# Where VectorE sums the w_down jobs: behind the gate of the tile whose loads theirs followed, in written order

## The chip, the cores and the metric

The kernel runs on one core of a Trainium2 chip. TensorE (PE) multiplies, ScalarE (ACT) and VectorE (DVE) work on tiles in on-chip memory, SyncE (SP) and GpSimd (POOL) issue the DMAs here, each in the order of its own queue. The metric is the device time of one launch in microseconds (us); lower is better. All engines run their instructions in the order that the scheduler gave them when the program was built. A line such as L881 is a line of the kernel before.

## The reference

One layer of a hybrid decoder in float32: 256 tokens, model width 2048.

```
h = RMSNorm(x);  z = h @ W_in             # split over three mixers
y = concat(pool_mixer, mla, memory_attn) @ W_o;  x = x + y
h2 = RMSNorm(x)
g = h2 @ W_gate                           # 2048 x 5632
gc = conv_b + sum_j conv_w[j] * shift(g)  # causal, width 3
x = x + (silu(gc) * (h2 @ W_up)) @ W_down # W_down: 5632 x 2048
```

The change touches only the last part, the gated feed-forward layer, and there the stage that makes gate and up.

## The kernel before, in words

Every float32 weight is split into a high part, rounded for TensorE, and a low part, the remainder. ScalarE makes the high part (`wh`, L102) and VectorE the low part (`wl`, L103, raw minus high). A product takes three rounds: high by high, high by low, low by high.

**The stage of gate and up.** The 5632 hidden features are 44 tiles of 128. For each tile f the program loads 1 MB of W_gate and 1 MB of W_up (`load_w`, L89, buffers `wr`, three of them in turn), splits each in two halves of 1024 columns (`wh` and `wl`, four buffers each), and runs 48 matmuls for gate and 48 for up (`gemm_pair`, L166). Gate runs its 32 high ones first and then its 16 low ones; up runs its 16 low ones first and then the 32 high ones. Tiles 1 to 43 go this way. "The start of tile f" below is its first gate matmul.

**The gate operations** (`glu`). VectorE scales the gate out of its accumulator (`g`, L827), ScalarE does the last tap of the convolution (L829), VectorE the other two (L831, twice), ScalarE the silu (L832), VectorE multiplies by up (L848, or L837 in pairs that are multiplied the plain way). Tiles are taken in pairs of an even and an odd one. Most pairs later go through a seven-product scheme: after the odd tile VectorE makes four sums (L852), ScalarE and VectorE split the result (L855, L856).

**The jobs.** The seven-product scheme needs four differences of blocks of W_down. For 28 pieces of 1 MB these are made during the gate and up stage, where the load queue has room: `job_load` (L874) issues the load of a piece into one of two buffers `wj` on SP's queue, `job_sums` subtracts on VectorE (L881, four instructions) and writes the result to a scratch tensor `tsum` with two DMAs on POOL's queue (L883). Job loads follow the loads of tiles 2, 3, 4, 6, 7, 9, 10, 12, 13, 15, 16, 17, 19, 20, 22, 23, 25, 26, 28, 29, 30, 32, 33, 35, 36, 38, 39 and 41. A `wj` buffer is free for the job after next as soon as its `tsum` DMAs have landed; so that job's load waits, on SP's queue, for these. After this stage the down stage (L929 to L931) reads the pieces of W_down and `tsum`.

**What sets the order.** A scheduler orders the instructions of each engine by when it reckons their inputs ready. `keep` pins an instruction behind the one that was written just before it on the same engine. The loads of tiles 1 to 43 and of the jobs are pinned on SP's queue: gate of f, up of f, the job's piece, gate of f+1. The operations of `glu` and `job_sums` are not pinned before the change, although `job_sums` of the piece loaded with tile f is written behind the `glu` of tile f+1.

Of the kernel before, what the change touches and what calls it, by code (L numbers as in the profile page):

```python
# [15 lines left out]
ALU = mybir.AluOpType  # L16
# [48 lines left out]
def layer(ctx, tc, xT_d, xn_d, memT_d, vec_d, tab_d, w_z_d, w_mqkr_d, w_q_d, w_kv_d, w_mem_d, w_pool_d, w_o_d,  # L65
          w_g_d, w_u_d, w_dn_d, out_d):
    nc = tc.nc
# [8 lines left out]
    def nm(s):  # L76
        uid[0] += 1
        return f"{s}_{uid[0]}"

    def ps_main():  # L80
        return psm.tile([P, 512], F32, tag="m", name=nm("psm"))
# [4 lines left out]
    def load_w(src, n, cut=STG, kept=False):  # L86
        raw = stage.tile([P, STG], F32, tag="wr", name=nm("wr"), bufs=3)
        for c in range(0, n, cut):
            keep(nc.sync.dma_start(raw[:, c:min(n, c + cut)], src[:, c:min(n, c + cut)]), kept)  # L89
        return raw[:]  # L90

    def keep(ins, on=True):

        return tc.keep_in_program_order(ins) if on else ins

    def split_w(raw, o, n, cut=HS, kept=False, shift=0):

        hi = stage.tile([P, HS + 64], F32R, tag="wh", name=nm("wh"), bufs=4)[:, shift:shift + HS]
        lo = stage.tile([P, HS + 64], F32R, tag="wl", name=nm("wl"), bufs=4)[:, shift:shift + HS]
        for c in range(0, n, cut):  # L100
            e = min(n, c + cut)
            keep(nc.scalar.copy(hi[:, c:e], raw[:, o + c:o + e]), kept)  # L102
            keep(nc.vector.tensor_tensor(lo[:, c:e], raw[:, o + c:o + e], hi[:, c:e].bitcast(F32), op=ALU.subtract),  # L103
                 kept)
        return hi, lo
# [7 lines left out]
    def rounds(act, k, low):  # L113

        m = act(k)
        h, l = (m[:, 0], m[:, 1]) if len(m.shape) == 3 else (m[:, 0:T], m[:, T:2 * T])
        return (h,) if low else (h, l)
# [37 lines left out]
    def gemm_pair(pss, raws, act):  # L155

        nk = HS // P
        for s, (ps, raw) in enumerate(zip(pss, raws)):


            parts = [split_w(raw, c * HS, HS, shift=16 if c else 48) for c in range(KD // nk)]
            for low in ((False, True) if s == 0 else (True, False)):
                for k in range(KD):
                    i = k % nk
                    for a, m in enumerate(rounds(act, k, low)):
                        nc.tensor.matmul(ps, parts[k // nk][low][:, i * P:(i + 1) * P], m,  # L166
                                         start=k + a == 0 and low == (s == 1), stop=k == KD - 1 and low == (s == 0),
                                         skip_group_check=True)
# [17 lines left out]
    def split_act(dst, src, scale=None, kept=False):  # L186


        h, l = (dst[:, 0], dst[:, 1]) if len(dst.shape) == 3 else (dst[:, 0:T], dst[:, T:2 * T])
        if scale is None:  # L190
            nc.scalar.copy(h, src)
            nc.vector.tensor_tensor(l, src, h.bitcast(F32), op=ALU.subtract)
        else:
            keep(nc.scalar.activation(h, src, AF.Copy, scale=scale), kept)
            keep(nc.vector.scalar_tensor_tensor(l, src, scale, h.bitcast(F32), op0=ALU.mult, op1=ALU.subtract), kept)
# [4 lines left out]
    def v(name, i=0):  # L200
        o = VOFF[name] + i
        return vec[:, o:o + 1]
# [323 lines left out]
    for m in range(6):  # L526
# [5 lines left out]
        a = zs[:, m // 4, :]  # L532
# [273 lines left out]
    r1 = const.tile([P, T], F32, name="r1")  # L806
# [17 lines left out]

    def glu(f, psg, psu, home=None):
        g = fp.tile([P, T], F32, tag="g", name=nm("g"), bufs=1)
        nc.vector.tensor_tensor(g[:], psg, r1[:], op=ALU.mult)  # L827
        gc = fp.tile([P, T], F32, tag="gc", name=nm("gc"), bufs=1)
        nc.scalar.activation(gc[:], g[:], AF.Identity, bias=v("conv_b", f), scale=v("cw2", f))  # L829
        for d, w in ((1, "cw1"), (2, "cw0")):  # L830
            nc.vector.scalar_tensor_tensor(gc[:, d:T], g[:, 0:T - d], v(w, f), gc[:, d:T], op0=ALU.mult, op1=ALU.add)  # L831
        nc.scalar.activation(gc[:], gc[:], AF.Silu)  # L832
        j, e = f // 2, f % 2
        if j not in SEVEN:
            if e == 0:
                aT[j] = fp.tile([P, 2, 2 * T], F32R, name=nm("aT"))
            nc.vector.tensor_tensor(gc[:], psu, gc[:], op=ALU.mult)  # L837
            split_act(aT[j][:, e, :], gc[:])
            return
        if e == 0:  # L840
            aT[j] = (home if j == PAIRS - 1 else away() if j in AWAY
                     else fp.tile([P, 14, P], F32R, name=nm("aS"))[:])
            hold[j] = fp.tile([P, 8, P], F32, tag="s8", name=nm("s8"), bufs=1)
        elif home is not None:
            aT[j] = home
        s = hold[j]
        o = 0 if e else 6
        nc.vector.tensor_tensor(s[:, o:o + 2, :].rearrange("p a t -> p (a t)"), psu, gc[:], op=ALU.mult)  # L848
        if e:
            for d, a, op, b in ((2, 7, ALU.add, 1), (3, 2, ALU.subtract, 6), (4, 6, ALU.subtract, 7),  # L850
                                (5, 0, ALU.subtract, 3)):
                nc.vector.tensor_tensor(s[:, d, :], s[:, a, :], s[:, b, :], op=op)  # L852
            hi, lo = (aT[j][:, i:i + 7].rearrange("p a t -> p (a t)") for i in (0, 7))
            sf = s[:, 0:7, :].rearrange("p a t -> p (a t)")
            nc.scalar.copy(hi, sf)  # L855
            nc.vector.tensor_tensor(lo, sf, hi.bitcast(F32), op=ALU.subtract)  # L856
            if j in AWAY:
                nc.gpsimd.dma_start(forms[:, AWAY.index(j)], aT[j])
# [4 lines left out]
    def away():  # L863
        return fp.tile([P, 14, P], F32R, tag="aL", name=nm("aL"), bufs=1)[:]
# [3 lines left out]
    def job_place():  # L868
        return fp.tile([P, STG], F32, tag="wj", name=nm("wj"), bufs=2)[:]

    def job_load(i):

        raw = job_place()
        keep(nc.sync.dma_start(raw, w_dn_d[SUMMED[i]]))  # L874
        return i, raw

    def job_sums(i, raw):

        r = raw.rearrange("p (b n) -> p b n", n=NN)
        for d, a, b in ((1, 0, 1), (0, 2, 0), (2, 2, 1), (3, 3, 2)):  # L880
            nc.vector.tensor_tensor(r[:, d], r[:, a], r[:, b], op=ALU.subtract)  # L881
        for h in range(2):
            nc.gpsimd.dma_start(tsum[:, i, h * HS:(h + 1) * HS], raw[:, h * HS:(h + 1) * HS])  # L883

    job_at = {2 + i * (KF - 5) // (len(SUMMED) - 1): i for i in range(len(SUMMED))}
    job = None

    raws = [load_w(w[0], STG) for w in (w_g_d, w_u_d)]
    pss = [ps_main()[:, 0:T] for _ in range(2)]
# [6 lines left out]
    for ps, raw in zip(pss, raws):  # L896
        gemm_t(ps, raw, HS, h2, range(8, KD), first=False)
    glu(0, *pss)
    for f in range(1, KF):
        pss = [ps_main()[:, 0:T] for _ in range(2)]  # L900
        gemm_pair(pss, [load_w(w[f], STG, kept=True) for w in (w_g_d, w_u_d)], h2)
        if f < KF - 1:
            glu(f, *pss)
        if job is not None:
            job_sums(*job)
        job = job_load(job_at[f]) if f in job_at else None

# [3 lines left out]
    dn = big.tile([P, 12, NN], F32, tag="act", name="dn")  # L913
    aS = big.tile([P, 14, P], F32R, tag="act2", name="aS")
    glu(KF - 1, *pss, aS[:])
    cnt = [0]

# [202 lines left out]
```

## Time and profile before

| what | value |
|---|---|
| median of three runs | 1013.21 us (1011.52 to 1016.26) |
| the profiled execution | 1012.18 us, span 1010.4 us |
| PE busy | 993.7 us, 98% |
| DVE busy | 785.0 us, 78% |
| ACT busy | 567.5 us, 56% |
| matmuls of L166, first start to last start | 303.9 to 788.4 us |
| DMA over the span | 292 GB/s |

The span is the profiled part of the launch; the rest of the launch's time (1.8 us here) lies around it. A busy share is an average over all stages. For this kernel it says that TensorE is the engine to look at, and that what can be won lies in the few us in which it stood still; which those are is read from the waits and the timeline.

### The profile page before, as it was taken

Reading aid. Unit: us, or ns where it says so; the run is one execution under the profiler, and the core shown is the slowest. Engines: PE = TensorE matmul, PEld = TensorE weight load, DVE = VectorE, ACT = ScalarE, POOL = GpSimd, SP = SyncE. Lnnn points to the kernel's source line nnn. Section 1 sums busy time; section 2 is a strip of 40 time slices with the busy share of each in tenths; the row PEclk is TensorE's granted clock in tenths of the full one; section 3 lists DMA queues with packets and bytes.
Section 4 is the critical chain, followed back from the end, with each engine's and each line's share of the span. In section 5 each row is a group of like instructions: output and inputs, shape, how many; then the busy total and the mean of one; then the engine's idle time right before and its main releaser. Section 6 shows DMA issues by size and latency. Waiting matters only on the chain.

```text
span 1010.4 us, 17323 instructions
## 1 busy us (share of the span) xinstructions
PE 993.7 (98%) x6870; PEld 917.5 (91%) x6870; DVE 785.0 (78%) x1174; ACT 567.5 (56%) x779; POOL 52.1 (5%) x102
## 2 busy tenths in 40 slices
PE   9999999999999999999999999999999999999998
PEld 7899988888889999999999999899999888888886
DVE  6878588765658687777878777777786889989887
ACT  7677666544555454444554444544455666757763
POOL 1100000000100000000000000000010000000000
PEclk9999999999999999999999999999999999999999
DMA  9867445334648799798998979898898999999992
GB/s 360 296 249 278 151 133 202 125 126 149 229 165 305 295 329 343 275 343 304 352 334 318 335 260 333 303 350 318 305 397 339 353 398 362 363 340 394 368 395 101
DMA packets 50578, 294.89 MB, mean 292 GB/s; under 512 B 5696, under 2 KB 6208, under 8 KB 25024
## 3 DMA queue, kind: packets, MB, share of 16 engines
q1 hardware_dynamic: 37728, 242.52, 65.9%
q0 software_dynamic: 12336, 50.47, 12.7%
q8 instruction: 54, 0.88, 0.3%
q10 hardware_dynamic: 432, 0.79, 0.3%
q14 instruction: 28, 0.23, 0.1%
HBM read 255.61 MB, written 38.14 MB: 291 GB/s over the span
## 4 chain that ended last, share of the span: by engine, by line
PE 66%; DVE 14%; DMA 14%; issue 3%; ACT 3%; SPq 0%; DVEq 0%; ACTq 0%
PE psm L166 17%; DMA wj<-in_w_dn 9%; DVE wl L103 8%; PE psm L182 5%; PE psm L184 5%; PE psm L183 5%; PE psm L149 4%; PE psa L931 4%; PE psm L931 4%; PE psa L930 4%; PE psa L929 4%; PE psm L930 4%; PE psm L929 4%; DMA tsum<-wj 2%; PE psm L133 2%
## 5 line engine op out<-in xcount | busy, mean ns | idle before, releaser
L103 DVE TENSOR_TENSOR wl<-wr,wh 128x1024 fp32r<-128x1024 f32 (+2 forms) x344 | 396.5, 1162 | 97.4 <-ACT wh L102 91.2
L102 ACT CAST wh<-wr 128x1024 fp32r<-128x1024 f32 (+2 forms) x344 | 336.0, 1000 | 130.1 <-PE psm L183 49.3
L166 PE MATMUL psm<-h,wh 128*128 128x256 f32 x2752 | 321.5, 277 | 2.1 <-ACT wh L102 2.1
L166 PEld LDWEIGHTS psm<-h,wh 128*128 128x128 f32 x2752 | 317.6, 189 | 2.3 <-ACT wh L102 2.3
L166 PE MATMUL psm<-h,wl 128*128 128x256 f32 x1376 | 169.0, 279 | 8.3 <-DVE wl L103 8.1
L166 PEld LDWEIGHTS psm<-h,wl 128*128 128x128 f32 x1376 | 161.8, 189 | 11.5 <-DVE wl L103 11.3
L881 DVE TENSOR_TENSOR wj<-wj 128x512 f32<-128x512 f32 x112 | 77.1, 688 | 56.0 <-DMA wj<-in_w_dn 54.5
L829 ACT ACTIVATE gc<-g,vec 128x256 f32<-128x256 f32 x44 | 26.5, 603 | 122.8 <-DVE g L827 122.8
L832 ACT ACTIVATE gc<-gc 128x256 f32<-128x256 f32 x44 | 18.4, 418 | 78.9 <-DVE gc L831 78.9
L102 ACT CAST wh<-wj 128x1024 fp32r<-128x1024 f32 (+1 forms) x48 | 47.1, 982 | 22.1 <-PE psa L930 11.6
L103 DVE TENSOR_TENSOR wl<-wj,wh 128x1024 fp32r<-128x1024 f32 (+1 forms) x48 | 53.7, 1133 | 6.3 <-ACT wh L102 2.4
L883 POOL DMA_DIRECT2D tsum<-wj x56 | 29.9, 534 | 398.8 <-DVE wj L881 335.4
L831 DVE SCALAR_TENSOR_TENSOR gc<-g,vec,gc 128x255 f32<-128x255 f32 x88 | 42.2, 479 | 1.3 <-ACT gc L829 0.7
L103 DVE TENSOR_TENSOR wl<-dn,wh 128x1024 fp32r<-128x1024 f32 (+1 forms) x36 | 40.1, 1133 | 3.4 <-ACT wh L102 1.7
L102 ACT CAST wh<-dn 128x1024 fp32r<-128x1024 f32 (+1 forms) x36 | 35.3, 982 | 10.7 <-PE psa L930 4.9
L182 PE MATMUL psm<-wh,cat 128*128 128x512 f32 x96 | 38.1, 397 | 0.0
L184 PE MATMUL psm<-wl,cat 128*128 128x512 f32 x96 | 37.4, 390 | 0.0
L183 PE MATMUL psm<-wh,cat 128*128 128x512 f32 x96 | 37.4, 389 | 0.0
L929 PE MATMUL psa<-wh,aS 128*128 128x512 f32 x84 | 32.7, 389 | 0.0
L930 PE MATMUL psm<-wh,aS 128*128 128x512 f32 x84 | 32.7, 389 | 0.0
L930 PE MATMUL psa<-wh,aS 128*128 128x512 f32 x84 | 32.7, 389 | 0.0
L929 PE MATMUL psm<-wh,aS 128*128 128x512 f32 x84 | 32.7, 389 | 0.0
(247 smaller groups left out, 1439.5 us busy)
## 6 DMA issues: line engine op xcount, KB each, us to landing
wr<-in_w_g SPq DMA_DIRECT2D x44, 1024.0 KB, 7.3
wr<-in_w_u SPq DMA_DIRECT2D x44, 1024.0 KB, 5.4
wj<-in_w_dn SPq DMA_DIRECT2D x32, 1024.0 KB, 8.7
tsum<-wj POOLq DMA_DIRECT2D x56, 512.0 KB, 7.8
wr<-in_w_o SPq DMA_DIRECT2D x16, 1024.0 KB, 4.8
wr<-in_w_dn SPq DMA_DIRECT2D x16, 768.0 KB, 7.1
wr<-tsum SPq DMA_DIRECT2D x12, 1024.0 KB, 7.3
wj<-tsum SPq DMA_DIRECT2D x12, 1024.0 KB, 7.0
```

The lines of the kernel that those rows point to most:

```text
L102: keep(nc.scalar.copy(hi[:, c:e], raw[:, o + c:o + e]), kept)
L103: keep(nc.vector.tensor_tensor(lo[:, c:e], raw[:, o + c:o + e], hi[:, c:e].bitcast(F32), op=ALU.subtract), kept)
L149: keep(nc.tensor.matmul(ps, parts[k // nk][low][:, i * P:(i + 1) * P], m, start=k + a == 0 and low == low_first, stop=k == KD - 1 and low ...
L166: nc.tensor.matmul(ps, parts[k // nk][low][:, i * P:(i + 1) * P], m, start=k + a == 0 and low == (s == 1), stop=k == KD - 1 and low == (s ...
L182: keep(nc.tensor.matmul(ps, xh, hi[:, i, o], start=first and i == 0, stop=False), kept)
L183: keep(nc.tensor.matmul(ps, xl, hi[:, i, o], start=False, stop=False), kept)
L184: keep(nc.tensor.matmul(ps, xh, lo[:, i, o], start=False, stop=last and i == nk - 1), kept)
L831: nc.vector.scalar_tensor_tensor(gc[:, d:T], g[:, 0:T - d], v(w, f), gc[:, d:T], op0=ALU.mult, op1=ALU.add)
L881: nc.vector.tensor_tensor(r[:, d], r[:, a], r[:, b], op=ALU.subtract)
L929: nc.tensor.matmul(ps, a[0], b[0], start=first, stop=False)
L930: nc.tensor.matmul(ps, a[1], b[0], start=False, stop=False)
L931: nc.tensor.matmul(ps, a[0], b[1], start=False, stop=last)
```

## The change

Three things are changed in the loop over the tiles. The first gate operation of every tile (`g`, L827) is pinned behind the instruction written before it, which is the tile's last low-part split. The four subtractions of a job are pinned, each behind the one before, and the first behind the last VectorE operation of `glu`. And `job_sums` of the piece that was loaded with tile f is written behind the `glu` of tile f itself, not of tile f+1; its load stands at the same place in SP's queue.

```diff
     def glu(f, psg, psu, home=None):
         g = fp.tile([P, T], F32, tag="g", name=nm("g"), bufs=1)
-        nc.vector.tensor_tensor(g[:], psg, r1[:], op=ALU.mult)
+        keep(nc.vector.tensor_tensor(g[:], psg, r1[:], op=ALU.mult))
...
         for d, a, b in ((1, 0, 1), (0, 2, 0), (2, 2, 1), (3, 3, 2)):
-            nc.vector.tensor_tensor(r[:, d], r[:, a], r[:, b], op=ALU.subtract)
+            keep(nc.vector.tensor_tensor(r[:, d], r[:, a], r[:, b], op=ALU.subtract))
...
     job_at = {2 + i * (KF - 5) // (len(SUMMED) - 1): i for i in range(len(SUMMED))}
-    job = None
...
         gemm_pair(pss, [load_w(w[f], STG, kept=True) for w in (w_g_d, w_u_d)], h2)
+        job = job_load(job_at[f]) if f in job_at else None
         if f < KF - 1:
             glu(f, *pss)
         if job is not None:
             job_sums(*job)
-        job = job_load(job_at[f]) if f in job_at else None
```

No instruction is added or taken away, and TensorE's order is the same. What moves is VectorE's order and, with it, ScalarE's and POOL's. The tile of a row is told by its buffers: the numbers rise with the program's text.

VectorE, before, around the sums of the job loaded with tile 13 (`wj_4852`), which has its first sum ahead of the gate split of tile 13 (`wr_4716`) and ahead of `g` of tile 12 (`psm_4584`):

```order
L881 TENSOR_TENSOR wj_4852<-wj_4852 128x512
L103 TENSOR_TENSOR wl_4721<-wr_4716,wh_4720 128x1024
L827 TENSOR_TENSOR g_4702<-psm_4584,r_2938 128x256
L103 TENSOR_TENSOR wl_4725<-wr_4716,wh_4724 128x1024
L831 SCALAR_TENSOR_TENSOR gc_4704<-g_4702,vec,gc_4704 128x255
L881 TENSOR_TENSOR wj_4852<-wj_4852 128x512
L831 SCALAR_TENSOR_TENSOR gc_4704<-g_4702,vec,gc_4704 128x254
L881 TENSOR_TENSOR wj_4852<-wj_4852 128x512 x2
L103 TENSOR_TENSOR wl_4777<-wr_4718,wh_4776 128x1024
```

VectorE, with the change, around the sums of the same job (`wj_4838`), which stand behind the pair's last operation (L856) and among the gate split of tile 15 (`wr_4990`) and `g` of tile 14 (`psm_4860`):

```order
L103 TENSOR_TENSOR wl_4923<-wr_4864,wh_4922 128x1024
L848 TENSOR_TENSOR s_661_4712<-psm_4721,gc_4842 128x256
L852 TENSOR_TENSOR s_661_4712<-s_661_4712 128x128
L103 TENSOR_TENSOR wl_4927<-wr_4864,wh_4926 128x1024
L852 TENSOR_TENSOR s_661_4712<-s_661_4712 128x128 x2
L856 TENSOR_TENSOR aS_4711<-s_661_4712,aS_4711 128x896
L881 TENSOR_TENSOR wj_4838<-wj_4838 128x512
L103 TENSOR_TENSOR wl_4995<-wr_4990,wh_4994 128x1024
L881 TENSOR_TENSOR wj_4838<-wj_4838 128x512
L827 TENSOR_TENSOR g_4978<-psm_4860,r_2938 128x256
L881 TENSOR_TENSOR wj_4838<-wj_4838 128x512
L103 TENSOR_TENSOR wl_4999<-wr_4990,wh_4998 128x1024
```

The sums of an odd tile's job have moved from the gate split of the tile itself to that of two tiles on; those of an even tile's job go to the up split of the next tile.

VectorE, before, where it makes the gate split of tile 18 (`wr_5400`) with `g` of tile 17 (`psm_5258`) between its halves:

```order
L852 TENSOR_TENSOR s_723_5248<-s_723_5248 128x128
L103 TENSOR_TENSOR wl_5325<-wr_5262,wh_5324 128x1024
L103 TENSOR_TENSOR wl_5405<-wr_5400,wh_5404 128x1024
L827 TENSOR_TENSOR g_5376<-psm_5258,r_2938 128x256
L103 TENSOR_TENSOR wl_5409<-wr_5400,wh_5408 128x1024
L831 SCALAR_TENSOR_TENSOR gc_5378<-g_5376,vec,gc_5378 128x255
```

The same place with the change (`wr_5406`, `psm_5264`), one of the three places where a job's load stands two tiles, not three, behind the load that used the same buffer:

```order
L881 TENSOR_TENSOR wj_5246<-wj_5246 128x512
L852 TENSOR_TENSOR s_724_5256<-s_724_5256 128x128
L881 TENSOR_TENSOR wj_5246<-wj_5246 128x512 x2
L827 TENSOR_TENSOR g_5384<-psm_5264,r_2938 128x256
L831 SCALAR_TENSOR_TENSOR gc_5386<-g_5384,vec,gc_5386 128x255
L831 SCALAR_TENSOR_TENSOR gc_5386<-g_5384,vec,gc_5386 128x254
L103 TENSOR_TENSOR wl_5411<-wr_5406,wh_5410 128x1024
L848 TENSOR_TENSOR s_724_5256<-psm_5265,gc_5386 128x256
```

Here the gate operations of tile 17 now stand ahead of the gate split of tile 18; the sums of job 16 stand ahead of both.

## The prediction

> **What bounds the kernel now.** I read the page first, for the engine that is busy all the time.
>
> ```profile
> span 1010.4 us, 17323 instructions
> PE 993.7 (98%) x6870; PEld 917.5 (91%) x6870; DVE 785.0 (78%) x1174; ACT 567.5 (56%) x779; POOL 52.1 (5%) x102
> ```
>
> TensorE bounds it, and only what makes it wait can be won. The change moves work in the gate and up stage alone, so the next view is TensorE's timeline there (start, duration, tile, count).
>
> ```profile
> 320.17 3.79 PE L166 MATMUL psm<-h,wl 128*128 128x256 f32 x32
> 323.80 7.42 PE L166 MATMUL psm<-h,wh 128*128 128x256 f32 x64
> 331.05 3.79 PE L166 MATMUL psm<-h,wl 128*128 128x256 f32 x32
> ...
> 781.25 3.79 PE L166 MATMUL psm<-h,wl 128*128 128x256 f32 x32
> ```
>
> From one low-part row to the next is an undisturbed tile: 331.05 - 320.17 = 10.88 us, of which 32 matmuls take 3.63 and 64 take 7.25. Gate is therefore 3.63 + 1.81 = 5.44 us and up another 5.44. The first row is tile 2, the last is tile 43: 461.08 us for 41 tiles that would need 446.08. So **15.0 us** are lost in this stage, and that is all the change can win. Next, who waits for whom between 316 and 789 us (total, times, longest).
>
> ```profile
> PE psm L166 <- DVE wl L103: 8.1, 10, 2.2
> ...
> DVE wj L881 <- DMA wj<-in_w_dn: 54.5, 15, 4.9
> ...
> SPq L874 <- DMA tsum<-wj: 10.5, 3, 7.5
> ```
>
> TensorE stands still for low parts alone, and VectorE waits longest for the job pieces. The timeline of tile 13, which starts at 438.55, shows how the two hang together.
>
> ```profile
> 428.65 0.37 SPq L874 DMA_DIRECT2D wj<-in_w_dn  x1
> ...
> 437.60 0.69 DVE L881 TENSOR_TENSOR wj<-wj 128x512 f32<-128x512 f32 x1 [3.44 <-DMA wj<-in_w_dn]
> 438.21 1.22 DVE L103 TENSOR_TENSOR wl<-wr,wh 128x1024 fp32r<-128x1024 f32 x1
> 439.35 0.42 DVE L827 TENSOR_TENSOR g<-psm,r 128x256 f32<-128x256 f32 x1
> ...
> 443.77 1.23 DVE L103 TENSOR_TENSOR wl<-wr,wh 128x1024 fp32r<-128x1024 f32 x1 [0.15 <-ACT wh L102]
> 445.05 1.21 PE L166 MATMUL psm<-h,wl 128*128 128x256 f32 x8 [0.90 <-DVE wl L103]
> 446.85 1.19 PE L166 MATMUL psm<-h,wl 128*128 128x256 f32 x8 [0.59 <-DVE wl L103]
> ```
>
> The first subtraction stands at the head of VectorE's queue before its piece is there (9 us after the issue). Behind it wait the gate split, `g`, all of the gate chain, then the up split at 443.77, which TensorE needs at 444.15 and has at 445.05. VectorE, not the load of weights, was late.
>
> **The change part by part.** Nothing is added; 112 subtractions and 56 stores move.
>
> *Removed: the waits for the pieces.* With the change a job's sums follow its own tile's `glu`. For tile 13 the piece has landed 1 us before the tile's start, and its sums come 16 us after it (laid out below). Even where a load is held up the piece is there 6 us early, but for job 17, which is about on time; so the 54.5 us go from VectorE. They cost TensorE the stalls that follow them, up to 15.0 us with what is lost around a stall.
>
> *Moved: the sums, hence the stores, hence the next load into the buffer.* This is the cost. I lay out one tile from the durations of the groups (mean ns behind the comma), zero being the start of tile f.
>
> ```profile
> L103 DVE TENSOR_TENSOR wl<-wr,wh 128x1024 fp32r<-128x1024 f32 x164 | 199.4, 1219 | 26.4 <-ACT wh L102 24.1 <-issue 2.3
> L102 ACT CAST wh<-wr 128x1024 fp32r<-128x1024 f32 x163 | 163.9, 1044 | 23.4 <-PE psm L166 18.6 <-DMA wr<-in_w_g 4.4
> L881 DVE TENSOR_TENSOR wj<-wj 128x512 f32<-128x512 f32 x111 | 76.4, 688 | 56.0 <-DMA wj<-in_w_dn 54.5
> L831 DVE SCALAR_TENSOR_TENSOR gc<-g,vec,gc 128x255 f32<-128x255 f32 x41 | 19.6, 478 | 0.0
> L852 DVE TENSOR_TENSOR s<-s 128x128 f32<-128x128 f32 x65 | 18.9, 290 | 1.6
> L827 DVE TENSOR_TENSOR g<-psm,r 128x256 f32<-128x256 f32 x41 | 17.1, 418 | 0.0
> L848 DVE TENSOR_TENSOR s<-psm,gc 128x256 f32<-128x256 f32 x33 | 13.8, 418 | 0.0
> L856 DVE TENSOR_TENSOR aS<-s,aS 128x896 fp32r<-128x896 f32 x11 | 12.0, 1093 | 11.2 <-ACT aS L855 11.2
> L855 ACT CAST aS<-s 128x896 fp32r<-128x896 f32 x11 | 10.4, 944 | 14.4 <-DVE s L852 14.4
> ```
>
> Gate ends at 5.4, `g` at 5.9, the second gate split of tile f+1 at 7.3. That split frees a weight buffer, so SP issues up of f+2 then, and wants to issue the job's piece right behind it. Up ends at 10.9, the product at 11.7. *Even tile:* four sums (2.75) with a split (1.22) and an L852 (0.29) among them end at 16.0. *Odd tile:* the up split of tile f+1 and the L852 first, then L855 and L856, to about 16; then the sums with two gate splits (2.44) and a `g` (0.42) among them, to 21.6. The store lands later by the first row below, that of the tsum issues (min/median/max); the others are the median landings of a gate load and of a piece:
>
> ```profile
> DMA to landing us min/median/max: 3.6/7.8/11.9
> ...
> wr<-in_w_g SPq DMA_DIRECT2D x44, 1024.0 KB, 7.3
> ...
> wj<-in_w_dn SPq DMA_DIRECT2D x32, 1024.0 KB, 8.7
> ```
>
> At 7.8, the buffer is free 23.8 us after an even tile's start and 29.4 after an odd one's. Most jobs' buffers are wanted again three tiles on, at 10.88 + 7.3 = 18.2. SP then waits 6 or 11 us, and everything behind the job on its queue waits too. What is behind it is the gate load of tile f+4, which its own buffer allows at 10.88 + 13.5 = 24.4 (the end of the up split that frees it; one tile earlier that is 11.7 + 0.6 + 1.22). After an even tile it isn't late. After an odd one it issues at 29.8, lands 7.3 later at 37.1, and must be there 1.04 (a ScalarE cast) before tile f+4 starts, at 43.52 - 1.04 = 42.5: late on the queue, hidden by 5.4 us of lead. Price zero, and the cover is that lead. (The job's own piece is issued at 29.4 and lands 8.7 later at 38.1; its sums start at 32.64 + 11.7 = 44.3 at the earliest, the 6 us named above.)
>
> Three times the buffer is wanted only two tiles on: job 4 after 2, 30 after 28 (even), 17 after 15 (odd). Then the gate load of f+3 has until 32.64 - 1.04 = 31.6. *Even:* issued at 24.2, it lands at 31.5, just in time; with SP's queue blocked little else moves, so the store should be nearer its minimum and the lead some us: zero. *Odd:* 29.8 + 7.3 = 37.1 is 5.5 us late; with the store at its minimum of 3.6, 21.6 + 3.6 + 0.4 + 7.3 = 32.9 is 1.3 late. I take the middle, **3.4 us** at the start of tile 18, since the stores of job 16 (sums to 10.9 + 16 = 27) run beside these loads. A standstill of this size has cost more than itself, as at tile 30:
>
> ```profile
> 630.95 1.98 PE L166 MATMUL psm<-h,wl 128*128 128x256 f32 x16
> 635.12 3.54 PE L166 MATMUL psm<-h,wl 128*128 128x256 f32 x16 [2.20 <-DVE wl L103]
> 638.46 7.87 PE L166 MATMUL psm<-h,wh 128*128 128x256 f32 x64
> 620.00:640.00 20.00, 17.80 (x137) 17.14 (x136) 14.94 (x22) 8.35 (x12) 1.61 (x3) 0.91 0.87 316
> ```
>
> After 2.20 us the same 16 matmuls took 3.54 instead of 1.98, the next 64 took 7.87 instead of 7.42, and the granted clock of the stretch was 0.91: **2.0 us** on top (bounds 0 and 2.0). The Trainium skill, "TensorE: Matmul & The Clock Gate", section "Part 1: The HAM clock gate", has the clock fall only after an idle window of about 3.4 us; by it a standstill of 2.2 us would lose nothing more, the trace disagrees here, and by the page the sum would be 2.0 us lower.
>
> The Trainium skill, "DMA: Bandwidth & Descriptors", section "Queues, rings and completion order", lets a DMA engine take turns between the queues that have work. By this the 1 MB of job 16's stores shares the engines with the late loads and the upper bound at tile 18 is nearer than the lower; the sum would be about 2 us higher.
>
> *VectorE with two jobs at once.* Where an odd job is followed by an even one (3-4, 9-10 and five more), VectorE gets eight sums in one tile: 4 x 1.22 + 0.42 + 2 x 0.48 + 0.42 + 2 x 0.29 = 7.3 of its own and 8 x 0.69 = 5.5 of sums, 12.8 in all, 1.9 more than 10.88. The lead of the up split is 5.0: TensorE frees its high buffer at 5.44 + 3.63 = 9.07, cast and split end at 11.3, and the low part is needed at 10.88 + 5.44 = 16.3. So the excess should be covered; but hand-overs between ScalarE and VectorE eat at this lead, and I put 1.0 us on it (bounds 0, and 7 times 0.59, the smaller stall in the rows above: 4.1).
>
> *ScalarE, POOL, the end.* ScalarE's few swaps follow VectorE's and lie under its idle 44%. On POOL the last job's second store stands behind the first fetch of the down stage; the load that reuses the buffer then comes at the start of that stage, some 3 us later than now, under a lead of one item. Zero, or at most the 3.
>
> **Sum**, against the profiled execution's own 1012.18: 1012.18 - 15.0 + 3.4 + 2.0 + 1.0 = 1003.6. The median of the runs shown is 1.0 higher than that execution, so **1004.5** for the median.
>
> **The rivals.**
>
> *A. No stall at tile 18.* The store lands fast and the gate load ahead of its time. For: the minimum of 3.6 was taken by the trace when little else moved. Against: even then the sum above is 1.3 late. Time: 1013.2 - 15.0 + 1 = about 999.
>
> *B. VectorE is short of time, not of data; the stalls stay.* For: this stall at 379.37 comes 21 us behind the last wait for a piece, and the stretch's own row (its third number is VectorE's) has VectorE busy for 367.9 us of 473, so that 50.6 are left beside the 54.5 of waits for pieces, for 43 tiles of waits for ScalarE:
>
> ```profile
> 358.51 0.69 DVE L881 TENSOR_TENSOR wj<-wj 128x512 f32<-128x512 f32 x1 [2.19 <-DMA wj<-in_w_dn]
> ...
> 379.37 1.20 PE L166 MATMUL psm<-h,wl 128*128 128x256 f32 x8 [0.44 <-DVE wl L103]
> ...
> 316.00:789.00 473.00, 464.75 (x4042) 461.41 (x4041) 367.86 (x540) 224.76 (x278) 33.10 (x62) 1.00 0.89 326
> ```
>
> Against: 54.5 us of waiting is as much as what was lacking. If half of the 15.0 stays and tile 18 costs 5.4: 1013.2 - 7.5 + 5.4 = about 1011, no change that can be told.
>
> *C. The blocked load queue becomes the bound: slower.* SP waits behind a job's store in each odd-tile case with three tiles between, eleven times. The lead there is 5.4 us. Store and gate load now take 7.8 + 7.3 in the median; from 20.5 us together TensorE waits at each. The store's maximum of 11.9 and this row of the weight loads allow it:
>
> ```profile
> DMA to landing us min/median/max: 3.6/5.7/10.6
> ```
>
> 11.9 + 10.6 is 2.0 late, and with the clock 4.0; at half of these places, 22: 1004.5 + 22 = about 1026. Against: while SP waits it loads nothing, and the store has the engines for itself.
>
> That the order doesn't move is excluded by the orders shown.
>
> **How the numbers follow.** Chances: the forecast 0.50, A 0.18, B 0.20, C 0.12. A measurement of this kernel can tell about 0.5%, 5 us: faster is below 1008.1, slower above 1018.3. The forecast's own range, from its bounds (tile 18 from 1.3 to 7.5, two jobs from 0 to 4.1), is 1013.2 - 15.0 + 1.3 = 999.5 to 1013.2 - 15.0 + 7.5 + 4.1 = 1009.8; of its chance 0.04 lies above 1008.1. So faster 0.46 + 0.18 = 0.64, same 0.24, slower 0.12. The range takes in A below and B above, and leaves C out: 998 to 1013.
>
> **What would show it.** Right: VectorE's wait for `wj` is near zero; SP's wait of L874 for the tsum stores grows from 10.5 us to between 100 and 250 (up to 6 us for an even job, 11 for an odd one, 18 for the three); the low-part rows are 10.88 apart nearly everywhere; TensorE waits once, at tile 18, for high parts of a late gate load. Wrong: stalls of L166 on `wl` that stay in tiles with two jobs (B); stalls on `wh` or gate loads every three or so tiles (C); or a down stage that begins to wait.

## The result

The changed kernel takes 1024.85 us (median of 4 runs, 1022.13 to 1029.38), the kernel before beside it 1014.74 us (1011.52 to 1016.27). The ratio is 1.0108, with a 95% interval of 1.0062 to 1.0155: about 1% slower, where 1004.5 us and a gain had been forecast. Two kernels that come out of the experiments below put the same subtractions at another place and take 995.8 us, 1.6% less than the kernel before.

### The profile page after: what moved, and what is told of

Its sections match the earlier page's. It is cut to its first block, busy times and chain, and to the rows that moved or that the text cites. A ratio compares the mean times of both kernels' runs of the same rounds, so it can differ in the third digit from the quotient of the medians.

```text
span 1020.4 us, 17361 instructions
## 1 busy us (share of the span) xinstructions
PE 994.7 (97%) x6870; PEld 918.8 (90%) x6870; DVE 784.2 (77%) x1174; ACT 568.5 (56%) x779; POOL 52.1 (5%) x102
## 4 chain that ended last, share of the span: by engine, by line
PE 55%; issue 28%; DMA 8%; DVE 5%; POOL 2%; ACT 1%; POOLq 0%; SPq 0%; DVEq 0%; ACTq 0%
PE psm L166 6%; PE psm L182 5%; PE psm L184 5%; PE psm L183 5%; PE psm L149 4%; DMA tsum<-wj 4%; PE psa L930 4%; PE psa L928 4%; PE psm L930 4%; PE psa L929 4%; PE psm L929 3%; PE psm L928 3%; DMA wr<-in_w_g 3%; DMA wj<-in_w_dn 2%; DVE wl L103 2%
## 5 line engine op out<-in xcount | busy, mean ns | idle before, releaser
L102 ACT CAST wh<-wr 128x1024 fp32r<-128x1024 f32 (+2 forms) x344 | 338.0, 1000 | 196.0 <-DMA wr<-in_w_g 62.9
L166 PE MATMUL psm<-h,wl 128*128 128x256 f32 x1376 | 167.8, 278 | 10.6 <-DVE wl L103 10.5
L930 PE MATMUL psm<-wl,aS 128*128 128x512 f32 x84 | 32.6, 392 | 1.3 <-DVE wl L103 1.3
L856 DVE TENSOR_TENSOR aS<-s,aS 128x896 fp32r<-128x896 f32 x12 | 13.1, 1092 | 26.7 <-ACT aS L855 26.7
L929 PE MATMUL psm<-wh,aS 128*128 128x512 f32 x84 | 32.7, 389 | 0.0
L929 PE MATMUL psa<-wh,aS 128*128 128x512 f32 x84 | 32.7, 389 | 0.0
```

The source lines that it names most:

```text
L929: nc.tensor.matmul(ps, a[1], b[0], start=False, stop=False)
L930: nc.tensor.matmul(ps, a[0], b[1], start=False, stop=last)
```

## The profile after

The profiled execution took 1022.13 us. Its page begins:

```profile
span 1020.4 us, 17361 instructions
PE 994.7 (97%) x6870; PEld 918.8 (90%) x6870; DVE 784.2 (77%) x1174; ACT 568.5 (56%) x779; POOL 52.1 (5%) x102
```

TensorE and VectorE do the work that they did before (993.7 and 785.0 us); the span grew by 10.0 us, by waits and by a slower clock behind them. These are the engines' waits between 316 and 800 us (us in total, times, longest):

```profile
DVE wl L103 <- ACT wh L102: 63.2, 36, 6.6
ACT wh L102 <- DMA wr<-in_w_g: 62.9, 20, 7.9
...
DVE aS L856 <- ACT aS L855: 25.7, 10, 7.2
...
PE psm L166 <- DVE wl L103: 10.5, 11, 1.5
...
PE psm L166 <- ACT wh L102: 5.8, 1, 5.8
```

SyncE's waits in the same stretch, and then the group of the subtractions from the page (its last number is VectorE's idle time ahead of them):

```profile
SPq L874 <- DMA tsum<-wj: 161.4, 26, 18.8
```

```profile
L881 DVE TENSOR_TENSOR wj<-wj 128x512 f32<-128x512 f32 x112 | 76.8, 686 | 0.9
```

The change removed what it was to remove: VectorE no longer waits for a piece (0.9 us of idle time, 56.0 before). In its place SyncE waits for the stores of the sums, 161.4 us instead of 10.5, and ScalarE waits for gate weights, 62.9 us instead of 4.4 in the row of the kernel before. How one leads to the other is seen ahead of tile 18. The rows are the timeline of all engines from 470 us on (start, duration, engine and line, and in brackets the idle time before):

```profile
471.02 0.33 SPq L874 DMA_DIRECT2D wj<-in_w_dn  x1
471.46 0.37 SPq L89 DMA_DIRECT2D wr<-in_w_g  x1
...
479.63 1.05 ACT L102 CAST wh<-wr 128x1024 fp32r<-128x1024 f32 x1 [7.90 <-DMA wr<-in_w_g]
480.58 0.94 ACT L855 CAST aS<-s 128x896 fp32r<-128x896 f32 x1
...
481.55 1.09 DVE L856 TENSOR_TENSOR aS<-s,aS 128x896 fp32r<-128x896 f32 x1 [7.19 <-ACT aS L855]
482.56 0.69 DVE L881 TENSOR_TENSOR wj<-wj 128x512 f32<-128x512 f32 x1
...
487.11 1.19 PE L166 MATMUL psm<-h,wl 128*128 128x256 f32 x8 [1.46 <-DVE wl L103]
488.22 0.53 POOL L883 DMA_DIRECT2D tsum<-wj  x1 [2.41 <-DVE gc L831]
...
491.23 0.33 SPq L874 DMA_DIRECT2D wj<-in_w_dn  x1
491.65 0.38 SPq L89 DMA_DIRECT2D wr<-in_w_g  x1
...
501.46 2.00 ACT L102 CAST wh<-wr 128x1024 fp32r<-128x1024 f32 x2 [4.98 <-DMA wr<-in_w_g]
502.56 6.28 PE L166 MATMUL psm<-h,wh 128*128 128x256 f32 x32 [5.81 <-ACT wh L102]
...
508.68 3.94 PE L166 MATMUL psm<-h,wl 128*128 128x256 f32 x32
```

Read it from the top. The piece of job 16 could be issued only at 471.02, when the stores of job 13 had landed, and the gate weights of tile 17 stand right behind it in the queue. They land at about 479.6, and ScalarE has stood still for 7.90 us for them. The cast of the forms of tiles 14 and 15 (L855) is behind that in ScalarE's order, VectorE's L856 needs it, and job 15's subtractions are pinned behind L856. So they begin at 482.56, 23.4 us into tile 15 (which began at 459.15), and end 28.5 us into it. Their second store is issued at 488.22 and has landed 2.9 us later. Then SyncE issues the next piece into that buffer (491.23, after the wait of 18.8 us in the row above) and then the gate weights of tile 18 (491.65), with two more weight loads behind them by 492.60. The gate weights take 9.7 us; ScalarE has them at 501.46 and TensorE has stood still for 5.81 us. **A late gate load made late subtractions, these a late store, and this the next late gate load.**

Tile by tile (the start of each tile's gate, less 10.88): tiles 2 to 11 lose nothing, then 0.8 us at tile 12, 1.9 at 14, 10.8 ahead of tile 18 (5.81, three short waits for low parts with 3.78 together, and the rest around them) and 2.7 behind it in slow matmuls, 0.9 at 34, 4.85 ahead of tile 38, 0.3 at 40. These make 22.3 us from tile 2 to the start of tile 43, where the kernel before lost 15.0. Tile 43 itself adds 2.7 and the first step of the down stage 1.3; the stage's start was 1.6 us better. 22.3 + 2.7 + 1.3 - 1.6 - 15.0 = 9.7, of the 10.0 by which the spans differ.

## The experiments

What lost the gain? **T1**: the round trip of a piece's buffer (load, subtractions, stores landed, next load), whose lateness SyncE's queue hands on to the gate weights behind it. **T2**: VectorE, which has too much pinned into tiles with two jobs. **T3**: the bytes of stores and loads, which collide. The order of the instructions answers one question by itself: with `keep` on the four subtractions alone every engine's order is that of the change, and with `keep` on `g` alone that of the kernel before. The pinned place of the subtractions is the whole change.

**Job 17 one tile later.** After `job_at`:

```diff
+    job_at[18] = job_at.pop(17)
```

> The edit moves one job from tile 17 to tile 18; the rest of the changed kernel stays. Three theories of why the changed kernel lost its gain. T1, the load queue: SyncE issues loads in order, a job's piece waits there for the stores of the job two before it, and the gate weights behind it come late; 15, 16, 17 is the place where two tiles lie between an odd job and the second next one, and it cost 10.8 us at tile 18 and 2.7 us of slow clock behind it. T2, VectorE: too much of its work is pinned into tiles with two jobs, and its low parts come late whatever the queue does. T3, bandwidth: loads and stores of these tiles collide, and all land late. T1 expects TensorE's 5.8 us wait for high parts at tile 18 gone and about 1024.85 - 13.5 = 1011 us (1008 to 1015), with the losses at tile 37 and at the stage's end unchanged. T2 and T3 expect the loss to move by a tile and the time to stay at 1020 or above.

1023.05 us (1021.19 to 1025.42), ratio 1.0108 (1.0070 to 1.0146): no gain. T1's number missed. The waits between 316 and 800 us, and SyncE's:

```profile
PE psm L166 <- DVE wl L103: 16.0, 16, 2.3
```

```profile
SPq L874 <- DMA tsum<-wj: 181.2, 26, 11.5
```

The standstill of 5.8 us is gone, and so is the longest wait of SyncE (11.5 instead of 18.8). But 23.4 us are still lost up to tile 43, now in more pieces: 4.8 ahead of tile 18, 3.1 at 20, 2.0 at 24, 2.9 at 28, 7.8 at 38. Sixteen short waits for low parts took the place of eleven and a long one. So the three jobs at 15, 16 and 17 are not the cause, only the place where it broke out. That the long standstill had let the chain of late loads catch up, and that it runs on without it, is my reading of the two tables; no run shows it alone.

**Pieces on GpSimd's queue.**

```diff
-        keep(nc.sync.dma_start(raw, w_dn_d[SUMMED[i]]))
+        keep(nc.gpsimd.dma_start(raw, w_dn_d[SUMMED[i]]))
```

> The edit issues the 28 pieces from GpSimd's queue, where the stores of the sums are issued, so that no weight load stands behind a piece any more. The same bytes move, and VectorE's pinned order stays. A piece now stands behind the stores of the job before it, so pieces come later, and VectorE may wait for them. T1 (load queue) expects SyncE's 161 us of waits for stores to be gone, TensorE's wait for high parts at tile 18 gone, and 1002 to 1012 us, the upper end if VectorE's wait for pieces comes back. T2 (VectorE) and T3 (bandwidth) expect 1020 us or more, with stalls where they were.

1039.29 us (1033.94 to 1042.00), ratio 1.0260 (1.0213 to 1.0308). T1's number missed by 27 us. SyncE's waits for stores are gone, as was said, but:

```profile
DVE wj L881 <- DMA wj<-in_w_dn: 51.9, 15, 6.8
...
PE psm L166 <- DVE wl L103: 21.1, 18, 3.3
```

A piece now stands behind the stores of the job before it, lands up to 27 us into its tile, and VectorE waits for it 51.9 us with the splits behind it, as it did for 54.5 us in the kernel before. The lateness was not cured but moved from one in-order queue to another. This run alone doesn't tell T1 from T2.

**Subtractions within the gate.**

```diff
         nc.scalar.activation(gc[:], gc[:], AF.Silu)
+        if job is not None:
+            job_sums(*job)
```

(and the call behind `glu` goes).

> The edit pins a job's four subtractions within its own tile's gate, behind its second L831 operation, instead of behind the whole gate: in the changed kernel's undisturbed tiles that is about 8 to 14 us into a tile's count and no longer 16 to 28, so stores are issued 5 to 14 us sooner. VectorE does the same work, the queues and bytes are the same. T1 (load queue) expects SyncE's waits for stores to fall from 161 us to under 40, no stall at tiles 18 and 37, and 998 to 1004 us. T2 (VectorE) expects the rest of the gate to be late in turn, with TensorE waiting for low parts in two-job tiles, and 1012 us or more. T3 (bandwidth) expects 1018 or more.

995.82 us (995.56 to 997.15), ratio 0.9840 (0.9801 to 0.9880): 2 us better than T1's range. From tile 2 to tile 43 0.2 us are lost. T2 and T3 fall as the only cause: VectorE has the same work and the same bytes move. SyncE's waits and ScalarE's:

```profile
SPq L876 <- DMA tsum<-wj: 78.0, 19, 10.7
```

```profile
ACT wh L102 <- DMA wr<-in_w_g: 8.6, 5, 4.3
```

T1 had expected under 40 us of SyncE's waits; there are 78.0, and they cost at most the 0.2. SyncE may wait as long as the gate weights behind it still come in time.

**Stores from another source.**

```diff
-            nc.gpsimd.dma_start(tsum[:, i, h * HS:(h + 1) * HS], raw[:, h * HS:(h + 1) * HS])
+            nc.gpsimd.dma_start(tsum[:, i, h * HS:(h + 1) * HS], h2s[0][:, 0, 0:4].rearrange('p a t -> p (a t)').bitcast(F32))
```

> The edit lets the stores read the same number of bytes from the FFN's input in SBUF instead of from the piece's buffer, so a piece's buffer comes free at the end of its four subtractions and no longer when the stores have landed (2.9 to 5 us later at the costly places). The sums themselves are left out of what is stored, so the down stage multiplies other numbers, in the same time. Stores, bytes and VectorE's work stay. T1 (load queue) expects the waits for stores on SyncE to turn into shorter waits for VectorE, the chain of late loads to shrink by 3 to 5 us for each link, the 5.8 us stall at tile 18 to fall to 2.5 us or less and the time to 1006 to 1016 us. T2 (VectorE) and T3 (bandwidth) expect no change, 1020 to 1028.

1007.59 us (1007.21 to 1009.80), ratio 0.9950 (0.9933 to 0.9967), within T1's range. But the test has a flaw: nothing bound these stores to the subtractions any more, and all 56 were through by 420 us, ahead of tile 12. While they ran, tile 2 began at 320.2 us instead of 315.0 and 6.4 us were lost at tile 6; from tile 13 on nothing is lost, but there was no store either. It does not tell T1 from T3.

**Half of the jobs early.** With the subtractions at the early place only in odd tiles:

```diff
-            glu(f, *pss)
-        if job is not None:
-            job_sums(*job)
+            if job is not None and f % 2:
+                glu(f, *pss, job=job)
+            else:
+                glu(f, *pss)
+                if job is not None:
+                    job_sums(*job)
```

> The edit pins the four subtractions early (behind the second L831 operation of their own tile's gate) for jobs in odd tiles alone; jobs in even tiles keep the changed kernel's place behind the gate. T1, sharpened by the runs so far: what is lost is the round trip of a piece's buffer (load, subtractions, stores landed, next load but one), whose lateness SyncE's queue hands on to the gate weights behind it. In the changed kernel an odd job's stores land 24 to 38 us into its tile's count and an even job's 18 to 30, and the next piece but one is due some 22 to 33 us after the job's tile begins, so the odd jobs alone carry the loss. T1 expects 997 to 1004 us and no stall at tiles 18 and 37. A theory by which each pinned job costs TensorE a like share, through VectorE's time or through collisions of bytes, expects about half of the gain, 1007 to 1013.

997.19 us (996.37 to 998.95), ratio 0.9836 (0.9821 to 0.9851); 1.3 us lost up to tile 43. And only in even tiles:

```diff
-            if job is not None and f % 2:
+            if job is not None and f % 2 == 0:
```

> The counterpart: jobs in even tiles early, jobs in odd tiles where the changed kernel has them. T1 expects the odd jobs' stores to be as late as before, and 1014 to 1024 us with the stalls of tiles 18 and 37 mostly there. A like share for each job expects 1007 to 1013.

1015.64 us (1010.83 to 1018.56), ratio 1.0022 (1.0004 to 1.0040); 14.3 us lost, with a standstill of 5.3 us ahead of tile 18 again. The odd jobs alone, whose stores are the latest, bring all but 1.4 us of the gain; the even ones alone bring some 9 us, so the two shares don't simply add. A like share for each job is excluded, and with it VectorE's load as such.

**Ahead of one operation.** In odd tiles that build forms:

```diff
+            if job is not None:
+                job_sums(*job)
             hi, lo = (aT[j][:, i:i + 7].rearrange("p a t -> p (a t)") for i in (0, 7))
...
```

> The edit moves the subtractions of jobs in odd tiles by one operation only, from behind L856, VectorE's operation on the tile pair's seven forms, which waits for ScalarE's cast of them, to ahead of it. VectorE's work is the same and its start in an undisturbed tile some 2 us sooner. In the changed kernel ScalarE stood 62.9 us before late gate weights with that cast behind it in its order, so a late gate load made the next subtractions late too. T1 with this feedback expects the chain to break up there: 1003 to 1013 us. If the lateness does not come round through ScalarE's cast, the gain is that of 2 us sooner stores, and 1015 to 1023 us.

1004.06 us (four executions: 999.77, 1001.42, 1006.70 and 1006.84), ratio 0.9905 (0.9869 to 0.9941): some 20 us come from one operation's place, 2 us in an undisturbed tile. In the traced execution (1001.42) 3.4 us are lost up to tile 43, and an odd job's subtractions begin 13.8 to 18.9 us into the tile. In the changed kernel they begin 13.6 to 23.4 us into it, and at 28.8 in tile 17, in which TensorE itself stood still. The time is what the feedback through ScalarE's cast was to give, and a larger gain than 2 us sooner stores were to; the two are not parted further. SyncE still waits 166.1 us for stores, so that total tells nothing of the loss.

**Stores with an eighth of the bytes.** The down stage reads a piece as it is in place of the sums.

```diff
-            nc.gpsimd.dma_start(tsum[:, i, h * HS:(h + 1) * HS], raw[:, h * HS:(h + 1) * HS])
+            nc.gpsimd.dma_start(tsum[:, i, h * HS:h * HS + P], raw[:, h * HS:h * HS + P])
...
-            sums = load_dn(tsum[:, SUMMED.index((c, j))])
+            sums = load_dn(w_dn_d[c, j])
```

> The edit stores 128 of each 1024 columns of the sums, so 7 of 8 stored bytes are left out in the gate and up stage; the down stage reads the unchanged piece in place of the sums, the same number of bytes, and multiplies other numbers. The piece's buffer still waits for its stores, VectorE's order is that of the changed kernel but for a few neighbouring operations. T3 (the bytes of the stores collide with loads) expects the loss gone, 1003 us or less. T1 (round trip) expects only the landing of the stores to be sooner, from 3 to 8 us down to about 2, with the subtractions as late as before: the waits of SyncE shrink by about a third and the time is 1008 to 1018 us.

995.56 us (995.42 to 997.03), ratio 0.9821 (0.9806 to 0.9835); nothing lost up to tile 43. T1's number missed, T3's was met. With the subtractions pinned where the changed kernel has them VectorE costs nothing (TensorE no longer waits for a low part between 316 and 800 us), and T2 is out for good. But two things are smaller here: the bytes, and the time until a store has landed. The next two runs part them.

**Bytes without the wait.** The stores, with 7 of 8 of their bytes, read a buffer of their own, which VectorE marks behind the subtractions:

```diff
+        fk = fks[i % 2]
+        keep(nc.vector.tensor_copy(fk[:, 0:1], raw[:, 0:1]))
...
-            nc.gpsimd.dma_start(tsum[:, i, h * HS:(h + 1) * HS], raw[:, h * HS:(h + 1) * HS])
+            nc.gpsimd.dma_start(tsum[:, i, h * HS:h * HS + 896].rearrange("p (a n) -> p a n", a=2),
+                                fk[:, None, :].to_broadcast([P, 2, 448]))
...
```

> The edit keeps the stores of the sums in their time and 7 of 8 of their bytes, but lets them read a buffer of their own (448 columns, read twice for each half), which VectorE marks behind the four subtractions by one more operation on one column. So the stores move when they did, and the piece's buffer comes free at the end of the subtractions. What is stored are not the sums, and the down stage reads the unchanged piece instead, the same bytes. T1 (round trip of the buffer: the stores' landing counts because the next load waits for it) expects 995 to 1003 us with no stall at tiles 18 and 37. T3 (the stores' bytes themselves slow the weight loads) expects the changed kernel's losses, 1012 us or more.

998.67 us (997.33 to 998.80), ratio 0.9862 (0.9843 to 0.9882); 1.4 us lost up to tile 43. The stores as the page lists them (KB each, median us to landing), and what SyncE's pieces wait for now:

```profile
tsum<-fk POOLq DMA_DIRECT2D x56, 448.0 KB, 9.2
```

```profile
SPq L874 <- DVE fk L883: 31.4, 12, 13.2
```

The stores landed later than in the changed kernel (9.2 us in the median, 6.4 there), up to 38 us into their tiles, and it cost at most the 1.4 us, with no load that waited for them.

**The wait with an eighth of the bytes.**

```diff
+        for k in range(2):
+            for h in range(2):
+                nc.gpsimd.dma_start(tsum[:, i, h * HS:h * HS + 32], raw[:, h * HS:h * HS + 32])
+            for h in range(2):
+                nc.gpsimd.dma_start(raw[:, h * HS:h * HS + 32], tsum[:, i, h * HS:h * HS + 32])
...
```

(in place of the two stores; the down stage again reads a piece as it is).

> The counterpart: 32 of each 1024 columns of the sums are stored, read back into the piece, stored and read back again, all on GpSimd's queue, so that a piece's buffer waits for a chain of four small transfers, some 8 to 10 us at about 2 to 2.5 us each, with an eighth of the bytes. The down stage reads the unchanged piece instead of the sums. With 128 columns stored once and not read back the changed kernel took 995.6 us. T1 (round trip) expects the loss back: SyncE's waits for the buffer at 150 us or more, stalls on high parts, 1008 to 1030 us. T3 (bytes) expects 994 to 1000 us.

1074.47 us (1072.51 to 1077.55), ratio 1.0617 (1.0591 to 1.0643). SyncE's and TensorE's waits between 316 and 800 us, and the small transfers of this stretch:

```profile
SPq L874 <- DMA wj<-tsum: 302.7, 29, 19.0
```

```profile
PE psm L166 <- ACT wh L102: 27.6, 12, 8.2
...
PE psm L166 <- DVE wl L103: 15.5, 29, 0.9
```

```profile
tsum<-wj POOLq DMA_DIRECT2D x104, 16.0 KB, 3.3
wj<-tsum POOLq DMA_DIRECT2D x102, 16.0 KB, 2.3
```

The sharpest picture of the mechanism: an eighth of the stores' bytes, VectorE's work unchanged, and 66 us lost up to tile 43, with twelve standstills for high parts. T1 had at most 1030, so its size was off; its direction and its row are there. The small transfers do not fill the DMA engines: these were busy 0.64 of the time from 316 to 760 us, and 0.84 in the changed kernel. T3 is out for stores spaced as they are here, but for at most the 1.4 us above: bytes slow a store's landing, but it is the waiting load that costs.

**Ahead of the gate.** In the loop over the tiles:

```diff
+        if job is not None:
+            job_sums(*job)
         if f < KF - 1:
             glu(f, *pss)
-        if job is not None:
-            job_sums(*job)
```

> The edit pins the subtractions of a job ahead of its tile's gate: some 2 to 5 us into the tile's count, between the place that VectorE had them at in the kernel before (at the landing of the piece, 3 us ahead of the tile's count to 5 behind it, 15 us lost) and that behind the second L831 (8.3 us, nothing lost). A piece lands 5 us ahead of to 4 us behind the tile's count. T1 expects VectorE to wait for some pieces again, by a few us each at most, and 995 to 1003 us, not better than the place behind the second L831 by more than can be measured.

995.77 us (995.67 to 997.35), ratio 0.9844 (0.9824 to 0.9864). Nothing is lost up to tile 43, no wait of VectorE for a piece is left, and SyncE's is down to this:

```profile
SPq L874 <- DMA tsum<-wj: 12.1, 3, 7.6
```

**The early place again**, with the edit of the subtractions within the gate.

> The kernel of the early place once more, with more rounds: all jobs' subtractions behind the second L831 of their own tile. Expected from its first runs: 994 to 998 us, ratio to the kernel before 0.980 to 0.988, and no loss in the gate and up stage beyond 1 us.

995.89 us (995.57 to 996.38), ratio 0.9838 (0.9819 to 0.9857). The two places can't be told apart; both are faster than both kernels of this case.

The runs side by side. The second column is where an odd job's subtractions begin, in us from its tile's start (of the change's jobs only that of tile 17 lies above 23.4); the fourth is the time lost from the start of tile 2 to that of tile 43 (the difference less 41 x 10.88). These and the waits are those of the traced execution; the median is of all:

| kernel | begin | SyncE waits for stores | lost | median |
|---|---|---|---|---|
| before | -2.9 to 0.8 | 10.5 | 15.0 | 1014.74 |
| ahead of the gate | 2.4 to 2.8 | 12.1 | 0.0 | 995.77 |
| within the gate | 8.3 to 8.5 | 78.0 | 0.2 | 995.82 |
| ahead of L856 | 13.8 to 18.9 | 166.1 | 3.4 | 1004.06 |
| the change | 13.6 to 28.8 | 161.4 | 22.3 | 1024.85 |

Too early, and VectorE waits for the piece; too late, and the buffer comes back late. Between them lie at least 6 us (2.4 to 8.5) in which the subtractions cost next to nothing.

## Why the prediction was wrong

**The removal was right.** The waits for pieces went from VectorE, and all of the 15.0 us can be won: two runs lose 0.0 and 0.2 in these tiles.

**The step that failed is the price of zero for a gate load behind an odd job, "hidden by 5.4 us of lead".** The lead was worked out from subtractions that end 21.6 us into their tile, whatever happens. I had SyncE's wait make gate weights late and stopped there. The trace goes round once more: ScalarE stands for these weights, the cast L855 is behind them in its order, L856 and the subtractions are behind the cast. For the first jobs the layout held: the subtractions of jobs 3 and 7 ended 20.0 and 22.2 us into their tiles. It lacked the way back, which the timeline shows from tile 9 on (this tile starts at 391.1), before TensorE has lost anything:

```profile
408.12 1.05 ACT L102 CAST wh<-wr 128x1024 fp32r<-128x1024 f32 x1 [4.85 <-DMA wr<-in_w_g]
409.07 0.94 ACT L855 CAST aS<-s 128x896 fp32r<-128x896 f32 x1
...
410.04 1.09 DVE L856 TENSOR_TENSOR aS<-s,aS 128x896 fp32r<-128x896 f32 x1 [4.99 <-ACT aS L855]
411.05 0.68 DVE L881 TENSOR_TENSOR wj<-wj 128x512 f32<-128x512 f32 x1
```

The gate weights of tile 11, late behind job 7's stores, hold up job 9's subtractions, which end at 25.0. Job 13's end at 25.9, and job 15's at 28.5, 6.9 us later than laid out: more than the lead of 5.4.

**Tile 18** was named as the one place with a stall on high parts, and it is. But 3.4 + 2.0 us became 10.8 + 2.7. The subtractions that set it ended 6.9 us later than laid out, which is the same omission. Store and gate load took 2.9 and 9.7 us, where the bounds had 3.6 to 7.8 and 7.3: together they lie inside the bounds. That a store is quick while SyncE waits was argued rightly; that four loads are then issued within 1.4 us (491.23 to 492.60), and the gate load lands later than its median, was not in the sum.

**The places priced at zero.** Tile 37 cost 4.85 us, in waits for low parts and slow matmuls behind them. The gate weights of tile 37 stand behind a piece that waited, and ScalarE waits for them, with the forms of tiles 34 and 35 and job 35's subtractions behind (they begin 22.0 us into tile 35); the low parts are late behind those:

```profile
710.24 1.05 ACT L102 CAST wh<-wr 128x1024 fp32r<-128x1024 f32 x1 [6.20 <-DMA wr<-in_w_g]
...
713.17 0.68 DVE L881 TENSOR_TENSOR wj<-wj 128x512 f32<-128x512 f32 x1
```

The end was "zero, or at most the 3" and cost 2.7 + 1.3: the piece of the down stage waits for stores (16.1 us on SyncE), the gate weights of tile 43 stand behind it, and ScalarE waits 6.24 us for those. Both are the same chain. The places ahead of tiles 12, 14, 34 and 40 add 3.9.

**VectorE with two jobs**, priced at 1.0, costs nothing by itself: the kernel of the small stores has the same order but for a few neighbouring operations, and loses nothing.

**The sum.** Against the 1003.6 us laid out for the profiled execution it took 1022.13, 18.5 more. Tile 18 gives 8.1 of this, tile 37 4.85, the end 4.0 and the four small places 3.9; VectorE's 1.0 falls away, and so do 1.6 at the stage's start, which have another cause (last section). That is 18.3.

**The rivals.** C, the blocked load queue, was the right one, at 0.12, and its argument was not: it asked whether a store and a gate load take 20.5 us together at their slowest, with the subtractions in their place, and spread the loss over eleven places. What decided was the time of the subtractions. That its 1026 us lie near the measured 1024.85 is luck. B's sign is there, eleven waits for low parts with 10.5 us, but B falls with the runs of small stores and of the early place, where VectorE has the same work and they are gone. A falls with the 5.81 us at tile 18. The sign to look for, SyncE's wait "between 100 and 250 us", was met at 161.4 and told nothing: with 166.1 another kernel lost 3.4 us. ScalarE's wait for gate weights goes nearer with the loss (62.9 us in the change, 8.6 in the early kernel), but it is no measure either: 52.3 us in the kernel that lost 3.4.

## What to carry to other kernels

When work on a double buffer is moved later, follow the lateness all the way round: buffer, load queue, what stands behind the load in that queue, and whether the moved work in its turn stands behind that. If the path closes, a lead that covers the first round doesn't cover the next ones. The place to look for here was neither the earliest nor the written end but the stretch between the piece's landing and the time from which the buffer's return delays another load; here moving four small operations there took 29 us off the changed kernel and 16 off the one before. A total of waits on a queue says little about what it costs; how late the subtractions come in their tile, read tile by tile, says more.

## What the runs showed of the hardware

**A standstill of one length costs differently.** At the start of the stage TensorE stands 2.14 us in both kernels. First the timeline row of the kernel before and its stretch from 300 to 320 us (the third number from the end is the granted clock), then those of the changed one:

```profile
303.92 5.54 PE L166 MATMUL psm<-h,wh 128*128 128x256 f32 x32 [2.14 <-ACT wh L102]
```

```profile
300.00:320.00 20.00, 17.86 (x143) 17.65 (x142) 13.92 (x19) 12.47 (x16) 0.00 (x0) 0.91 0.61 244
```

```profile
303.91 3.98 PE L166 MATMUL psm<-h,wh 128*128 128x256 f32 x32 [2.14 <-ACT wh L102]
```

```profile
300.00:320.00 20.00, 17.86 (x156) 17.65 (x156) 13.28 (x18) 13.37 (x17) 0.00 (x0) 1.00 0.62 252
```

The same matmuls behind the same standstill took 5.54 us at a granted clock of 0.91 and 3.98 at 1.00: this is the 1.6 us by which the stage began better. It is none of the change's doing: the standstill belongs to tile 1, and the first job to tile 2. Of the fourteen traces here thirteen have it, with 2.14 or 2.15 us; the granted clock from 300 to 320 us is 0.91 in five of them and 1.00 in eight. The Trainium skill, "TensorE: Matmul & The Clock Gate", section "Part 1: The HAM clock gate", has the clock follow a free-running window of activity; that one standstill can cost 1.6 us or nothing agrees with it, though 2.14 us is less than the about 3.4 us that it gives this window. After 5.81 us ahead of tile 18 the clock fell as well (0.59 granted from 502.5 to 508.7 us): 32 matmuls took 6.28 us and the next 3.94, where 3.79 is the usual.

**A store's landing has a part that bytes don't explain.** In the median 16 KB took 3.3 us to land in memory and 2.3 us to come back (the rows above), 64 KB took 3.3 in the run of small stores, and 512 KB 6.4 in the changed kernel. The quickest took 1.7 us (16 KB), 1.8 (64 KB) and 2.9 (512 KB). The Trainium skill, "DMA: Bandwidth & Descriptors", section "Anatomy of one DMA — SWDGE (gpsimd) path", puts the fixed part at about 2 us, most of it the confirmation from the target memory. The quickest small stores here agree; the medians, taken beside other traffic, are above it. A buffer that waits for its store pays this in any case, and the run with four of them in a row shows what that is worth.
